# Up products of three of eleven pairs of inner tiles as seven products of halves

## The chip, the cores and the metric

The kernel runs on one core of one Trainium2 chip. The metric is the device time of one execution in microseconds (us), the median of several runs. The core has a matrix engine (TensorE: PE for its products, PEld for its weight loads), a vector engine (VectorE, DVE), a scalar engine (ScalarE, ACT), GpSimd (POOL) and SyncE (SP), which issues the transfers.

## The reference, cut to what matters

One decoder layer on 512 tokens of width 1024: forgetting attention with 16 heads, layer norm, a gated MLP with a causal convolution, layer norm, and a gated embedding. The change lies in the MLP:

```python
def conv_ffn(x, w_up, conv_w, conv_b, w_down):      # x: 512 x 1024, FFN_DIM = 2816
    u, g = jnp.split(x @ w_up, [FFN_DIM], axis=-1)
    g = causal_dwconv(g, conv_w, conv_b)             # three taps along the tokens
    return (jax.nn.gelu(g, approximate=False) * u) @ w_down
```

## The kernel before, in words

Every operand of a product is float32 and is cut into a high and a low part (`whi`, `wlo`); `three` (L113, its matmul is L118) makes one product from three matmuls: high by high, high by low, low by high. Each matmul loads its own 128 x 128 weights.

`Weights` holds all weights of the kernel as one list of units in the order of their use. `load_to` (L70) issues a unit's transfer into one of four `raw` buffers; `cut_to` (L83) makes the high part on ACT (L96) and the low part on DVE (L97), into one of five pairs of split buffers; `get(i, 2)` asks for unit i with two more cut ahead of it. A unit may have a `make` function, which builds sums or differences of its blocks on DVE before the cut, with a second block that comes by its own transfer into a tile `side`.

The MLP has 22 inner tiles f of 128 columns, that is 11 pairs j = (2j, 2j+1). For each f, `up(f, 0)` computes the gate product g and `up(f, 1)` the product u: 8 blocks of 128 rows by three matmuls of 512 tokens, 24 matmuls in all, into one PSUM buffer (two buffers with the tag "two" from f = 6 on; the other six hold the down products). Only f = 0 and the gate of f = 1 go in halves of 256 tokens. `conv` (L572) reads g on ACT and DVE, and `product` (L583) multiplies by u into E, a tile of quarters of the pair's activations. After the second tile of a pair, `operands` (L588) makes four sums of the quarters on DVE and cuts seven quarters at once into `hh` and `hl` (L599, L600).

The down products of pairs 0 to 8 are already made as seven products of halves (the phases in `down`, L602), with the activations as the weights and 512 columns moving. Part p of the loop (L645) does the up products of six inner tiles; between them, `between` (L653) puts steps of the down products of the part before. A step is two products of 6 matmuls (one product in the last phase). What a phase has finished is added to y on DVE by `add_half` (L498, L501, L503), which frees its PSUM buffer. Pairs 9 and 10 (part 3) are done plainly at the end, in the stage r.

`flip` (L520) transposes x1, the normed input of the MLP, on PE into x1h and x1l.

The tile framework orders each engine's instructions when the program is built and inserts the waits; an instruction that waits holds up what stands behind it on its engine.

Of the kernel before, what the change touches and what calls it, by code (L numbers as in the profile page):

```python
# [9 lines left out]
F32 = mybir.dt.float32  # L10
F32R = mybir.dt.float32r
# [5 lines left out]
P = 128  # L17
# [12 lines left out]
REST = range(18, 22)  # L30

CHUNKS = (None, (1,) * 12, (1,) * 12, (2, 1) * 4)
HALF = S // 2
ALPHA = 2.0 ** 0.25
EPS = 1e-5
# [73 lines left out]
def trunk_layer(ctx: ExitStack, tc: tile.TileContext, xT, x2d, pT, wqk, wv0, wv1, wv2, bf, wo, wup, cwb,  # L109
# [44 lines left out]

    side = {}

    def down_units(part):
        def b_rows(j, k0, n, cols):  # L160
            return half_rows(wdn, 2 * j + k0, n, cols)

        def t12(j, i):
            def make(t):
                if t is None:
                    if part not in side:
                        side[part] = base.tile([P, 6, 512], F32, tag="xl", name=f"side{part}")
                    nc.sync.dma_start(side[part][:, i, :], wdn[2 * j * P:(2 * j + 1) * P, 0:512])
                    return None
                t1, t2 = t[:, :512], side[part][:, i, :]  # L170
                nc.vector.tensor_sub(t1, t1, t2)
                nc.vector.tensor_sub(t2, t[:, 512:], t1)
                return [t1, t2]
            return make

        def t3(t):
            if t is None:
                return None
            nc.vector.tensor_sub(t[:, :512], t[:, 512:], t[:, :512])
            return [t]  # L180

        def t4(i):
            def make(t):
                if t is None:
                    return None
                nc.vector.tensor_sub(t[:, :512], t[:, :512], side[part][:, i, :])
                return [t[:, :512]]
            return make

        js = PAIRS[part]  # L190
        return [(b_rows(j, 0, 2, 0), UNIT, None) for j in js] + \
            [(b_rows(j, 0, 2, 1), UNIT, t12(j, i)) for i, j in enumerate(js)] + \
            [(b_rows(j, 0, 2, 1), UNIT, t3) for j in js] + \
            [(b_rows(j, 1, 1, 0), 512, t4(i)) for i, j in enumerate(js)]

    u_up, u_dn = {}, [[] for _ in PAIRS]
    for part in range(4):
        fs = range(6 * part, min(6 * part + 6, NF))
        todo = down_units(part - 1) if part else []
        for i, (f, q) in enumerate((f, q) for f in fs for q in range(2)):  # L200
            u_up[f, q] = W.add(wup[f, 1 - q], inner=P)
            for _ in range(CHUNKS[part][i] if part else 0):
                if todo:
                    src, n, make = todo.pop(0)
                    u_dn[part - 1].append(W.add(src, n=n, inner=512, make=make))
# [311 lines left out]
        nc.vector.scalar_tensor_tensor(y[:, t], y[:, t], mv[:, 0:1], g, op0=ALU.subtract, op1=ALU.mult)  # L517
        nc.vector.scalar_tensor_tensor(y[:, t], y[:, t], mv[:, 3:4], b, op0=ALU.mult, op1=ALU.add)

    def flip(t, xh, xl):  # L520

        for n in range(2):
            ps = bank("nt")
            for k in range(4):
                nc.tensor.transpose(ps[:, k * P:(k + 1) * P],
                                    y[:, t, (4 * n + k) * P:(4 * n + k + 1) * P], ident)
            dst = slice(4 * n, 4 * n + 4), slice(t * P, (t + 1) * P)
            ps3 = ps.rearrange("p (k c) -> p k c", c=P)
            nc.scalar.activation(xh[:, dst[0], dst[1]], ps3, AF.Copy)
            nc.vector.tensor_sub(xl[:, dst[0], dst[1]], ps3, xh[:, dst[0], dst[1]].bitcast(F32))  # L530

    x1h = post.tile([P, KD, S], F32R, tag="xh", name="x1h")
    x1l = post.tile([P, KD, S], F32R, tag="xl", name="x1l")
    rows = ExitStack()
    rpool = rows.enter_context(tc.tile_pool(name="rows", bufs=1))
    g1, b1 = [row(rpool.tile([P, D], F32, name=n), src) for n, src in (("g1", gm), ("b1", bm))]
# [5 lines left out]
    for t in range(NT):  # L542
        ps = bank(f"ap{t}")
        tk = slice(t * P, (t + 1) * P)
        for k in range(KD):
            hi, lo = W.get(u_o[1][k // 2])
            c = slice(k % 2 * 512, k % 2 * 512 + 512)
            three(ps, hi[:, c], lo[:, c], oh[:, k, tk], ol[:, k, tk], k == 0, k == KD - 1,
                  weights_move=True)
            if t > 1 and k == 3:  # L550
                flip(t - 2, x1h, x1l)
        add_half(t, 1, ps, True)
        half_stats(t, 1)
        norm(t, g1, b1, (2, x1h, x1l) if t == 3 else None)
    rows.close()
    oT.close()

# [27 lines left out]

    gates = {}

    def operands(hh, hl, i, E):  # L588
# [10 lines left out]
        nc.scalar.activation(hh[:, i], E[:, HALF:], AF.Copy)  # L599
        nc.vector.tensor_sub(hl[:, i], E[:, HALF:], hh[:, i].bitcast(F32))  # L600

    def down(part, hh, hl):  # L602
# [4 lines left out]
        A11, A22, A12, S1, S2, S3, S4 = range(7)  # L607
        acc = {(b, i): bank(f"{b}{part}{i}", "six") for b in "yzx" for i in range(2)}
        seen, opened = set(), set()

        def chain(b, a, us, col, n):

            j, u = us[n]
            hi, lo = W.get(u, 2)
            last = n == k - 1
            c = slice(col * 512, col * 512 + 512)
            for i in range(2):
                tk = slice(a * HALF + i * P, a * HALF + (i + 1) * P)
                on = (b, i) in opened
                three(acc[b, i], hi[:, c], lo[:, c], hh[:, j, tk], hl[:, j, tk], n == 0 and not on,  # L620
                      last, weights_move=True, on=on)
                if last:
                    opened.add((b, i))
# [19 lines left out]

    before = None
    for part in range(4):  # L645
        if part < 3:
            shape = [P, len(PAIRS[0]), 7 * HALF]
        else:
            shape = [P, len(REST), S]
        hh, hl = [hpool.tile(shape, F32R, tag=g, name=f"{g}{part}", bufs=2) for g in ("hh", "hl")]  # L650
        slots = iter(CHUNKS[part] or ())

        def between():  # L653
            for _ in range(next(slots, 0)):
                next(before)

        for f in range(6 * part, min(6 * part + 6, NF)):
            q, j = f % 2, f // 2
            if q == 0:
                E = hpool.tile([P, 8 * HALF], F32, tag="E", name=f"E{j}")  # L660
            if f == 0:
                a, b = slice(0, HALF), slice(HALF, S)
                up(0, 0, a)
                up(0, 1, a)
                up(1, 0, a, (3, x1h, x1l))
# [6 lines left out]
            if f > 1:  # L672
                up(f, 0)
            conv(f)
            between()
            up(f, 1)
            product(f, E[:, q * S:(q + 1) * S])
            if q:
                if part < 3:
                    operands(hh, hl, j - 3 * part, E)  # L680
                else:
                    i = f - 1 - REST[0]
                    e = E[:, :2 * S].rearrange("p (a b) -> p a b", b=S)
                    nc.scalar.activation(hh[:, i:i + 2], e, AF.Copy)
                    nc.vector.tensor_sub(hl[:, i:i + 2], e, hh[:, i:i + 2].bitcast(F32))
            between()
        if part < 3:
            before = down(part, hh, hl)
# [4 lines left out]
    for g in ("hh", "hl"):  # L693
        extra.append(hpool.tile([P, 3, UNIT], F32R, tag=g, name=f"{g}p", bufs=2))
    for i, t in enumerate(tiles):
        tk = slice(t * P, (t + 1) * P)
        for n in range(2):
            ps = bank(f"r{t}_{n}", "six")
            for k in range(len(REST)):
                hi, lo = W.get(u_r[n][k // 2])  # L700
                c = slice(k % 2 * 512, k % 2 * 512 + 512)
                three(ps, hi[:, c], lo[:, c], hh[:, k, tk], hl[:, k, tk], k == 0, k == len(REST) - 1,
                      weights_move=True)
            add_half(t, n, ps, False)
            half_stats(t, n)
# [108 lines left out]
```

## Time and profile before

| | |
|---|---|
| median of 3 runs | 660.29 us (660.05 to 661.29) |
| the profiled execution | 662.73 us, of which the span from first to last instruction is 661.0 us |
| busy in the span: PE, PEld | 653.7 us (99%), 556.8 us (84%) |
| busy in the span: DVE, ACT, POOL | 474.6 us (72%), 309.5 us (47%), 84.2 us (13%) |
| granted TensorE clock | 0.996 of full speed |
| DMA | 76.95 MB, mean 116 GB/s |

A busy PE is read from pipelined records, so that 99% says that matmuls follow each other without holes, not that each runs at its peak. Idle time of an engine that isn't the bottleneck costs nothing. The MLP's up and down products run from 249 to 576 us.

### The profile page before, as it was taken

Reading aid. Unit: us, or ns where it says so; the run is one execution under the profiler, and the core shown is the slowest. Engines: PE = TensorE matmul, PEld = TensorE weight load, DVE = VectorE, ACT = ScalarE, POOL = GpSimd, SP = SyncE. Lnnn points to the kernel's source line nnn. Section 1 sums busy time; section 2 is a strip of 40 time slices with the busy share of each in tenths; the row PEclk is TensorE's granted clock in tenths of the full one; section 3 lists DMA queues with packets and bytes.
Section 4 is the critical chain, followed back from the end, with each engine's and each line's share of the span. In section 5 each row is a group of like instructions: output and inputs, shape, how many; then the busy total and the mean of one; then the engine's idle time right before and its main releaser. Section 6 shows DMA issues by size and latency. Waiting matters only on the chain.

```text
span 661.0 us, 8683 instructions
## 1 busy us (share of the span) xinstructions
PE 653.7 (99%) x3234; PEld 556.8 (84%) x3234; DVE 474.6 (72%) x746; ACT 309.5 (47%) x511; POOL 84.2 (13%) x78
## 2 busy tenths in 40 slices
PE   8999999999999999999999999999999999999997
PEld 6899888888888889888888888888888888888886
DVE  6574789988896597755677675777657766599364
ACT  5543777877776223534434333443425343426231
POOL 0000544454446020000000000000000000012000
PEclk8999999999999999999999999999999999999999
DMA  8533211122153213323344244533363433562221
GB/s 281 168 125 115 82 46 54 65 65 65 37 208 125 98 36 125 128 97 95 98 140 146 95 160 128 159 128 112 100 199 117 125 133 125 159 224 66 101 81 48
DMA packets 32890, 76.95 MB, mean 116 GB/s; under 512 B 2960, under 2 KB 6800, under 8 KB 32848
## 3 DMA queue, kind: packets, MB, share of 16 engines
q1 hardware_dynamic: 32848, 76.41, 36.0%
q8 instruction: 25, 0.41, 0.3%
q14 instruction: 17, 0.14, 0.1%
HBM read 74.17 MB, written 2.10 MB: 115 GB/s over the span
## 4 chain that ended last, share of the span: by engine, by line
PE 97%; DMA 1%; ACT 1%; SPq 0%; issue 0%; DVE 0%
PE g L118 18%; PE u L118 18%; PE pp L118 13%; PE x L118 7%; PE pv L118 7%; PE gt L118 7%; PE z L118 4%; PE ao L118 3%; PE r L118 3%; PE ap L118 3%; PE o L408 3%; PE t L395 2%; PE y L118 2%; PE pl L118 2%; PE s L364 2%; PE s L366 1%
## 5 line engine op out<-in xcount | busy, mean ns | idle before, releaser
L96 ACT ACTIVATE whi<-raw 128x1024 fp32r<-128x1024 f32 (+5 forms) x131 | 126.3, 964 | 190.5 <-PE g L118 64.4
L97 DVE TENSOR_TENSOR wlo<-raw,whi 128x1024 fp32r<-128x1024 f32 (+5 forms) x131 | 143.3, 1099 | 67.4 <-ACT whi L96 67.0
L382 POOL TENSOR_SCALAR pr<-pr,rl 128x128 f32<-128x128 f32 (+1 forms) x64 | 71.9, 1141 | 138.1 <-DVE rl L378 138.1
L118 PE MATMUL g<-x1h,whi 128*128 128x512 f32 (+1 forms) x192 | 71.5, 372 | 0.0
L118 PE MATMUL g<-x1l,whi 128*128 128x512 f32 (+1 forms) x192 | 71.3, 371 | 0.0
L118 PE MATMUL g<-x1h,wlo 128*128 128x512 f32 (+1 forms) x192 | 71.3, 371 | 0.0
L118 PE MATMUL u<-x1h,whi 128*128 128x512 f32 (+1 forms) x184 | 69.9, 380 | 0.0
L118 PE MATMUL u<-x1l,whi 128*128 128x512 f32 (+1 forms) x184 | 69.9, 380 | 0.0
L118 PE MATMUL u<-x1h,wlo 128*128 128x512 f32 (+1 forms) x184 | 69.9, 380 | 0.0
L514 POOL TENSOR_TENSOR mv<-mv,neghalf 128x1 f32<-128x1 f32 x8 | 11.6, 1446 | 382.6 <-DVE mv L513 360.3
L118 PE MATMUL pp<-xh,wlo 128*128 128x512 f32 x128 | 50.5, 394 | 0.0
L118 PE MATMUL pp<-xl,whi 128*128 128x512 f32 x128 | 50.0, 390 | 0.0
L118 PE MATMUL pp<-xh,whi 128*128 128x512 f32 x128 | 49.9, 390 | 0.0
L374 ACT ACTIVATE pr<-s,nm 128x128 f32<-128x128 f32 (+1 forms) x64 | 33.4, 524 | 17.4 <-DVE nm L373 14.3
L118 PEld LDWEIGHTS g<-x1h,wlo 128*128 128x128 f32 x192 | 36.2, 188 | 6.3
L118 PEld LDWEIGHTS g<-x1l,whi 128*128 128x128 f32 x192 | 36.2, 188 | 6.2
L118 PEld LDWEIGHTS g<-x1h,whi 128*128 128x128 f32 x192 | 36.1, 188 | 6.2
L584 DVE TENSOR_TENSOR E<-a,u 128x512 f32<-128x512 f32 x22 | 15.1, 686 | 35.8 <-PE u L118 35.1
L118 PEld LDWEIGHTS u<-x1h,wlo 128*128 128x128 f32 x184 | 34.6, 188 | 6.6
L118 PEld LDWEIGHTS u<-x1h,whi 128*128 128x128 f32 x184 | 34.6, 188 | 6.5
L118 PEld LDWEIGHTS u<-x1l,whi 128*128 128x128 f32 x184 | 34.6, 188 | 6.5
L118 PE MATMUL pv<-whi,xh 128*128 128x384 f32 (+1 forms) x96 | 30.6, 331 | 1.9 <-ACT whi L96 1.9
(173 smaller groups left out, 1420.0 us busy)
## 6 DMA issues: line engine op xcount, KB each, us to landing
raw<-wup SPq DMA_DIRECT2D x44, 512.0 KB
raw<-wdn SPq DMA_DIRECT2D x31, 512.0 KB
raw<-wqk SPq DMA_DIRECT2D x16, 512.0 KB
raw<-wo SPq DMA_DIRECT2D x8, 512.0 KB
raw<-wg SPq DMA_DIRECT2D x8, 512.0 KB
raw<-wv SPq DMA_DIRECT2D x8, 384.0 KB
side<-wdn SPq DMA_DIRECT2D x9, 256.0 KB
raw<-wdn SPq DMA_DIRECT2D x9, 256.0 KB
```

The source lines that it names most:

```text
L96: self.nc.scalar.activation(hi[:, c:e], piece, AF.Copy)
L97: self.nc.vector.tensor_sub(lo[:, c:e], piece, hi[:, c:e].bitcast(F32))
L118: nc.tensor.matmul(ps, lhsT, rhs, start=start and n == 0, stop=stop and n == 2, skip_group_check=on)
L364: nc.tensor.matmul(ps[:, :n], QA[:, q], KA[:, :n], start=True, stop=False)
L366: nc.tensor.matmul(ps[:, :n], qb[0:68, q], kb[0:68, :n], start=False, stop=True)
L374: nc.scalar.activation(pr[:, off:off + w], ps[:, :w], AF.Exp, bias=nm[:, i:i + 1], accum_out=ls[:, i:i + 1])
L382: nc.gpsimd.tensor_scalar_mul(pr[:, off:off + w], pr[:, off:off + w], rl[:, i:i + 1])
L395: nc.tensor.transpose(ps[:, w:w + P], pr[:, o:o + P], ident)
L408: nc.tensor.matmul(ps[:, q0:], V[:, j, h], p[:, o:o + w], start=j == 0 and n == 0, stop=j == NT - 1 and n == 1)
L514: nc.gpsimd.tensor_tensor(mv[:, 3:4], mv[:, 2:3], neghalf, op=ALU.pow)
L584: nc.vector.tensor_mul(e, gates.pop(f), ups.pop((f, 1)))
```

## The change

For the pairs j = 4, 7 and 9, the two gate products (and likewise the two u products) are made as one 2 x 2 block product by Strassen's scheme in Winograd's form: the blocks are two halves of the 1024 rows by the two inner tiles for the weights, and two halves of the tokens by two halves of the rows for x1. Seven block products of 4 x 3 matmuls with 256 moving tokens take the place of eight. The sums of x1's blocks are made once, after f = 1 (`x_sums`), from an uncut copy of x1^T which `flip` now also writes (`whole`), and stay resident in `xs`. The sums of the weights' blocks are made by DVE in the units' `make` functions (`up_units`). A pair's seven products go in four stages of `up_step`, first for s = 0 (the gate), then for s = 1, with steps of the down products between them; partial sums leave PSUM by ACT (c1, c2) and return by DVE additions into E. `conv` and `product` of these pairs read E.

The down products' operands lie in three kinds of tiles (A, B, S) by how long they live instead of `hh` and `hl`, so that `operands` cuts them by three instructions on each engine instead of one. The tile `side` is one for the whole kernel.

```diff
+UP_PAIRS = (4, 7, 9)
...
+    def up_units(j):
+        f0, f1 = 2 * j, 2 * j + 1
+
+        def unit(f, q, make=None, k0=0):
+            return W.add(wup[f, 1 - q][:, k0:], n=(KD - k0) * P, inner=P, make=make)
+
+        return (lambda q: unit(f0, q), lambda q: unit(f1, q, t12(wup[f0, 1 - q][:, :4], 3 + q)),
+                lambda q: unit(f1, q, t3), lambda q: unit(f0, q, t4(3 + q), 4))
...
-        for i, (f, q) in enumerate((f, q) for f in fs for q in range(2)):
-            u_up[f, q] = W.add(wup[f, 1 - q], inner=P)
+        for i in range(2 * len(fs)):
+            f, q = fs[i // 2], i % 2
+            j, n = f // 2, i % 4
+            if j in UP_PAIRS:
+                stages = up_units(j)
+                for st, sq in (((0, 0),), ((0, 1),), ((1, 0), (1, 1)), ((2, 0), (2, 1)))[n]:
+                    u_up[j, st, sq] = stages[st](sq)
+            else:
+                u_up[f, q] = W.add(wup[f, 1 - q], inner=P)
...
+            if j in UP_PAIRS and n == 3:
+                for sq in range(2):
+                    u_up[j, 3, sq] = stages[3](sq)
...
-    def flip(t, xh, xl):
+    def flip(t, xh, xl, whole=None):
...
+        for k, ps3 in halves if whole is not None else ():
+            nc.scalar.activation(whole[t][:, k, :], ps3, AF.Copy)
...
+    def x_sums():
...
+        for i in range(2):
+            nc.vector.tensor_add(s(0, i), blk(2 + i, 0), blk(2 + i, 1))
+            nc.vector.tensor_sub(s(1, i), s(0, i), blk(i, 0))
+            nc.vector.tensor_sub(s(2, i), blk(i, 0), blk(2 + i, 0))
+            nc.vector.tensor_sub(s(3, i), blk(i, 1), s(1, i))
+        for n in range(4):
+            k = slice(4 * n, 4 * n + 4)
+            nc.scalar.activation(xs[0][:, k, :], sums[n], AF.Copy)
+            nc.vector.tensor_sub(xs[1][:, k, :], sums[n], xs[0][:, k, :].bitcast(F32))
+
+    def up_step(j, st, s, E):
+        if st == 0:
+            ups[j, s] = bank(f"{'gu'[s]}{2 * j}", "two" if j > 2 else None)
+        ps = ups[j, s]
+        z, x = ps[:, :HALF], ps[:, HALF:]
+        hi, lo = W.get(u_up[j, st, s], 2)
...
+        def go(to, col, on, a=None, sn=None, last=4):
+            for k in range(4):
+                w = slice((4 * col + k) * P, (4 * col + k + 1) * P)
+                if a is None:
+                    mh, ml = [v[:, 4 * sn + k, :] for v in xs]
+                else:
+                    mh, ml = [v[:, a[0] + k, a[1]] for v in (x1h, x1l)]
+                three(to, hi[:, w], lo[:, w], mh, ml, k == 0 and not on, k == 3, on=on)
...
+        if st == 0:
+            go(z, 1, False, a=(4, first))
+            go(x, 0, True, a=(0, first))
+            nc.scalar.activation(c1, z, AF.Copy)
+            nc.scalar.activation(z.rearrange("p (a b) -> p a b", b=P),
+                                 zeros.unsqueeze(1).to_broadcast([P, 2, P]), AF.Copy)
+            nc.vector.tensor_add(e[:, :HALF], x, c1)
+        elif st == 1:
+            go(z, 0, True, sn=0)
+            go(x, 1, True, sn=1)
+            nc.scalar.activation(c2[:, :HALF], x, AF.Copy)
+            nc.scalar.activation(c2[:, HALF:], z, AF.Copy)
+        elif st == 2:
+            go(z, 1, True, sn=3)
+            go(x, 0, True, sn=2)
+            nc.vector.tensor_add(e[:, S:], ps, c2)
+        else:
+            go(x, 0, True, a=(4, second))
+            nc.scalar.activation(e[:, HALF:S], x, AF.Copy)
+            del ups[j, s]
...
+            if j in UP_PAIRS:
+                if q == 0:
+                    up_step(j, 0, 0, E)
+                    between()
+                    up_step(j, 0, 1, E)
+                    between()
+                    continue
+                for st in (1, 2):
+                    up_step(j, st, 0, E)
+                    up_step(j, st, 1, E)
+                    if st == 1:
+                        between()
+                conv_product(f, E)
+                between()
+                up_step(j, 3, 0, E)
+                up_step(j, 3, 1, E)
+                conv_product(f - 1, E)
...
+            if f == 1:
+                x_sums()
```

## Rows read from the trace of the kernel before

**Rows 1.** The page, part 1: engine, busy us, share of the span, instructions.
```profile
PE 653.7 (99%) x3234; PEld 556.8 (84%) x3234; DVE 474.6 (72%) x746; ACT 309.5 (47%) x511; POOL 84.2 (13%) x78
```
**Rows 2.** The page, part 4: the chain that ended last, by engine.
```profile
PE 97%; DMA 1%; ACT 1%; SPq 0%; issue 0%; DVE 0%
```
**Rows 3.** Windows of whole pairs: length, busy us (instructions) of each engine, clock, DMA.
```profile
316.56:349.20 32.64, 32.64 (x146) 27.03 (x145) 24.87 (x36) 12.96 (x17) 0.00 (x0) 1.00 0.37 114
349.20:381.84 32.64, 32.64 (x146) 27.03 (x145) 22.18 (x29) 12.25 (x14) 0.00 (x0) 1.00 0.35 114
381.84:410.40 28.56, 28.56 (x128) 23.65 (x127) 17.04 (x22) 11.72 (x14) 0.00 (x0) 1.00 0.52 164
443.04:475.68 32.64, 32.64 (x146) 27.03 (x145) 22.27 (x29) 12.25 (x14) 0.00 (x0) 1.00 0.36 114
504.24:542.32 38.08, 38.08 (x170) 31.53 (x169) 28.81 (x40) 15.40 (x19) 0.00 (x0) 1.00 0.42 131
542.32:576.32 34.00, 34.00 (x152) 28.15 (x151) 21.67 (x28) 12.98 (x16) 0.00 (x0) 1.00 0.44 136
```
**Rows 4.** Waits from 316.56 to 576.32: who waited for whom, us, times, longest.
```profile
ACT whi L96 <- PE g L118: 51.5, 15, 4.8
ACT whi L96 <- PE u L118: 51.0, 17, 4.8
```
**Rows 5.** Timeline of PE, first and last matmul of the first half of u0.
```profile
252.31 0.28 PE L118 MATMUL u<-x1h,whi 128*128 128x256 f32 x1
...
255.07 0.28 PE L118 MATMUL u<-x1h,wlo 128*128 128x256 f32 x1
```
**Rows 6.** Timeline of PE: first matmul of a gate product and what follows its 24.
```profile
349.20 0.39 PE L118 MATMUL g<-x1h,whi 128*128 128x512 f32 x1
...
354.64 0.39 PE L118 MATMUL z<-whi,hh 128*128 128x512 f32 x1
```
**Rows 7.** The page, part 5: one group of weight loads.
```profile
L118 PEld LDWEIGHTS g<-x1h,wlo 128*128 128x128 f32 x192 | 36.2, 188 | 6.3
```
**Rows 8.** Groups of DVE by line and form: busy us, mean ns, idle before.
```profile
L97 DVE TENSOR_TENSOR wlo<-raw,whi 128x1024 fp32r<-128x1024 f32 x99 | 120.1, 1218 | 55.8 <-ACT whi L96 55.5
L600 DVE TENSOR_TENSOR hl<-E,hh 128x1792 fp32r<-128x1792 f32 x9 | 18.2, 2021 | 5.9 <-ACT hh L599 5.9
...
L97 DVE TENSOR_TENSOR wlo<-raw,whi 128x512 fp32r<-128x512 f32 x18 | 12.3, 685 | 5.6 <-ACT whi L96 5.6
L503 DVE TENSOR_TENSOR y<-y,x 128x512 f32<-128x512 f32 x18 | 12.0, 680 | 0.0
...
L171 DVE TENSOR_TENSOR raw<-raw,side 128x512 f32<-128x512 f32 x9 | 6.2, 690 | 7.0 <-DMA raw<-wdn 7.0
...
L598 DVE TENSOR_TENSOR E<-E 128x256 f32<-128x256 f32 x9 | 3.8, 423 | 0.2
```
**Rows 9.** Groups of ACT by line and form.
```profile
L96 ACT ACTIVATE whi<-raw 128x1024 fp32r<-128x1024 f32 x99 | 104.9, 1059 | 133.4 <-PE g L118 50.1 <-PE u L118 26.7 <-PE z L118 9.0
...
L307 ACT ACTIVATE V<-pv 128x256 fp32r<-128x256 f32 x4 | 1.4, 420 | 0.0
```
**Rows 10.** Timeline of ACT where the gate product of rows 6 ends.
```profile
354.61 1.06 ACT L96 ACTIVATE whi<-raw 128x1024 fp32r<-128x1024 f32 x1 [2.78 <-PE g L118]
355.58 0.76 ACT L576 ACTIVATE a<-g,cw 128x512 f32<-128x512 f32 x1
```
**Rows 11.** Timelines of SP and of DVE: a transfer's issue, and what waited for it.
```profile
332.69 0.38 SPq L77 DMA_DIRECT2D raw<-wdn  x1
...
336.57 0.69 DVE L171 TENSOR_TENSOR raw<-raw,side 128x512 f32<-128x512 f32 x1 [1.22 <-DMA raw<-wdn]
```
**Rows 12.** Windows, columns as in rows 3: from u2 to u5, and in stage r.
```profile
278.48:316.56 38.08, 38.08 (x170) 31.53 (x169) 21.58 (x25) 14.32 (x17) 0.00 (x0) 1.00 0.30 97
576.32:592.82 16.50, 16.50 (x73) 13.39 (x72) 16.21 (x23) 4.59 (x5) 1.46 (x1) 1.00 0.70 231
```

More of the change, by code (lines that the diff above doesn't have):

```diff
@@ L153, in trunk_layer, with side, t12, make @@
     u_o = [[W.add(half_rows(wo, 2 * j, 2, n), inner=512) for j in range(4)] for n in range(2)]
-    side = {}
+    aside = []
+    def side(i):
+        if not aside:
+            aside.append(base.tile([P, 8, 512], F32, tag="xl", name="side"))
+        return aside[0][:, i, :]
+    def t12(b11, i):
+        def make(t):
+            if t is None:
+                to = side(i)
+                if len(b11.shape) == 3:
+                    to = to.rearrange("p (a b) -> p a b", b=P)
+                nc.sync.dma_start(to, b11)
+                return None
+            t1, t2 = t[:, :512], side(i)
+            nc.vector.tensor_sub(t1, t1, t2)
+            nc.vector.tensor_sub(t2, t[:, 512:], t1)
+            return [t1, t2]
+        return make
+    def t3(t):
+        if t is None:
+            return None
+        nc.vector.tensor_sub(t[:, :512], t[:, 512:], t[:, :512])
+        return [t]
+    def t4(i):
+        def make(t):
+            if t is None:
+                return None
+            nc.vector.tensor_sub(t[:, :512], t[:, :512], side(i))
+            return [t[:, :512]]
+        return make
     def down_units(part):
@@ L518, in norm @@
         nc.vector.scalar_tensor_tensor(y[:, t], y[:, t], mv[:, 3:4], b, op0=ALU.mult, op1=ALU.add)
-    def flip(t, xh, xl):
+    def flip(t, xh, xl, whole=None):
+        halves = []
         for n in range(2):
@@ L530, in flip, with cut_tiles @@
             nc.vector.tensor_sub(xl[:, dst[0], dst[1]], ps3, xh[:, dst[0], dst[1]].bitcast(F32))
+            halves.append((dst[0], ps3))
+        for k, ps3 in halves if whole is not None else ():
+            nc.scalar.activation(whole[t][:, k, :], ps3, AF.Copy)
     x1h = post.tile([P, KD, S], F32R, tag="xh", name="x1h")
     x1l = post.tile([P, KD, S], F32R, tag="xl", name="x1l")
+    post.tile([P, 48], F32, name="lead")
+    spool = ctx.enter_context(tc.tile_pool(name="spool", bufs=1))
+    def cut_tiles(kind, n, bufs, name, dtype=F32R, pool=spool):
+        return [pool.tile([P, n, HALF], dtype, tag=f"{kind}{g}", name=f"{name}{g}", bufs=bufs) for g in "hl"]
+    xt, sums = {}, []
+    for t in range(NT):
+        a, b = cut_tiles("S", 4, 4, f"x1t{t}", F32)
+        xt[t] = a.rearrange("p a (b c) -> p (a b) c", c=P)
+        sums.append(b)
     rows = ExitStack()
@@ L586, in trunk_layer, with blk, s @@
     gates = {}
-    def operands(hh, hl, i, E):
+    xs = cut_tiles("X", 16, 1, "xs", pool=hpool)
+    def x_sums():
+        def blk(t, k):
+            return xt[t][:, 4 * k:4 * k + 4, :]
+        def s(n, i):
+            return sums[n][:, :, i * P:(i + 1) * P]
+        for i in range(2):
[7 more added lines that the diff above has]
+            nc.vector.tensor_sub(xs[1][:, k, :], sums[n], xs[0][:, k, :].bitcast(F32))
@@ L591, in e, with conv_product, operands @@
+    def conv_product(f, E):
+        c = slice(f % 2 * S, f % 2 * S + S)
+        ups[f, 0], ups[f, 1] = E[:, 2 * S:][:, c], E[:, c]
+        conv(f)
+        product(f, E[:, c])
+    def operands(ops, E):
         def e(n):
@@ L616, in chain @@
             c = slice(col * 512, col * 512 + 512)
+            xh, xl = ops[j][a[0]]
             for i in range(2):
-                tk = slice(a * HALF + i * P, a * HALF + (i + 1) * P)
+                tk = slice(i * P, (i + 1) * P)
                 on = (b, i) in opened
-                three(acc[b, i], hi[:, c], lo[:, c], hh[:, j, tk], hl[:, j, tk], n == 0 and not on,
+                three(acc[b, i], hi[:, c], lo[:, c], xh[:, a[1], tk], xl[:, a[1], tk], n == 0 and not on,
                       last, weights_move=True, on=on)
@@ L645, in trunk_layer @@
     for part in range(4):
[L646 to L650, printed above, removed]
+        ops = []
         slots = iter(CHUNKS[part] or ())
@@ L671, in trunk_layer @@
                 continue
[L672 to L677, printed above, removed]
+            if j in UP_PAIRS:
[15 more added lines that the diff above has]
+                conv_product(f - 1, E)
+            else:
+                if f > 1:
+                    up(f, 0)
+                conv(f)
+                between()
+                up(f, 1)
+                product(f, E[:, q * S:(q + 1) * S])
+            if f == 1:
+                x_sums()
             if q:
                 if part < 3:
-                    operands(hh, hl, j - 3 * part, E)
-                else:
[L682 to L686, printed above, removed]
+                    ops.append([cut_tiles("A", 2, 3, f"a{j}"), cut_tiles("B", 1, 5, f"b{j}", pool=hpool),
+                                cut_tiles("S", 4, 4, f"s{j}")])
+                    operands(ops[-1], E)
+                else:
+                    h, l = cut_tiles("S", 4, 4, f"s{j}")
+                    e = E[:, :2 * S].rearrange("p (a b) -> p a b", b=HALF)
+                    nc.scalar.activation(h, e, AF.Copy)
+                    nc.vector.tensor_sub(l, e, h.bitcast(F32))
+                    ops.append((h, l))
+            if j not in UP_PAIRS:
+                between()
         if part < 3:
-            before = down(part, hh, hl)
+            before = down(part, ops)
     gb = hpool.tile([P, 2, D], F32, tag="E", name="g2b2")
```

59 lines of the change are left out of this document (21 added, 38 removed).

## The prediction

> **What bounds the kernel now.** I read the page's first part, then the chain that ended last, then windows of single pairs. PE is busy in 99% of the span [rows 1] and makes 97% of the chain [rows 2]; in every window of the MLP its busy time is the window itself, at the full clock of 2.4 GHz [rows 3]. So a saved PE microsecond is a saved microsecond as long as nothing else takes its place, and every stall of PE counts in full. Next comes DVE: in the windows of j = 3, 4, 7, 9 and 10 it is busy 24.87 of 32.64, 22.18 of 32.64, 22.27 of 32.64, 28.81 of 38.08 and 21.67 of 34.00 us [rows 3]. Idle DVE there isn't lateness. The longest waits of the MLP are ACT's, for PE to give back a split buffer (51.5 and 51.0 us in 32 times) [rows 4]: cutting runs as far ahead as five split buffers allow, one in use and four ready. That lead is what the change will draw on.
>
> **PE's part.** In halves of 256 tokens, 24 matmuls follow each other at (255.07 - 252.31) / 23 = 0.120 us [rows 5]. With 512 tokens 24 take 354.64 - 349.20 = 5.44 us, 0.2267 each [rows 6]. The columns alone are 106.7 and 213.3 ns at 2.4 GHz, so each matmul has 13.3 ns on top, whatever its width. A pair before: 2 tiles x 2 products x 24 = 96 wide matmuls, 21.76 us. After: 2 x 7 x 12 = 168 narrow ones, 20.16 us. An eighth fewer columns would be 2.72 us, but 72 more matmuls take 0.96 back; 1.60 us are left, in three pairs 4.80. This is the only time removed from the path. The down products have the same number and width of matmuls.
>
> The narrow row above has its own weight load for each matmul, and was taken while DVE was busy too. The Trainium skill ("TensorE: Matmul & The Clock Gate", "Back-to-back issue gap") gives a lone warm matmul N / 2.4 + 2.5 ns. By that a pair would go from 20.72 to 18.35 us, and the three would save 7.1. The trace doesn't agree: it has 13.3 ns where the page has 2.5, and I take the row.
>
> **DVE's part, in a changed pair.** Durations from [rows 8]: a plain unit's low part 1.22 us, 512 columns 0.685, a sum of 512 columns 0.69, of 256 0.42. Before, four up units took 4 x 1.22 = 4.87. After, for each of g and u: stage 0 1.22; stage 1 two sums and two cuts, 2.75; stage 2 a sum and a full cut, 1.91; stage 3 a sum and half a cut, 1.37; together 7.25, for both 14.50, so 9.6 more. The partial sums into E add 2 x 0.42 + 2 x 0.69 = 2.2. Three operand cuts in place of one of 2.02 cost 0.685 + 0.42 + 1.22 = 2.3, so 0.3 more (not for j = 9, which has no such operands). Pairs 4, 7 and 9 then need 34.3, 34.4 and 40.6 us of DVE, and PE takes 31.04, 31.04 and 36.48. DVE is over by 3.3, 3.4 and 4.2: in these pairs it, not PE, is the slower engine. Whether that shows is a question of the lead.
>
> I followed it for j = 4 by hand, from PE's start of stage 0 as time 0. Order of use: A (stage 0, s = 0), a down step, B, a down step d5, C and D (stage 1), d6, E and F (stage 2), d7, G and H (stage 3); PE gives A to F 2.88 us each, G and H 1.44, a down step 2.72. Five split buffers mean that A, B and the first down step are cut at 0. The last u product of j = 3 ended at -2.72; its product and operands (0.69 + 1.7 + 2.3 us) hold DVE until 2.0. Then DVE finishes d5 at 4.7, C (with A's addition to E) at 7.9, D at 10.6, d6 (with B's) at 12.9, four additions to y (0.68 each) at 15.7, E at 17.6, F at 19.5, d7 at 21.4, G at 22.8, H at 24.1. PE wants C at 11.2, D 14.1, d6 17.0, E 19.7, F 22.6, d7 25.4, G 28.2, H 29.6. The least margin is 2.1 us, at E; each cut here also starts after its buffer is free. For j = 9 (two down steps, then one, in turn) the same gives E finished at 23.6 and wanted at 25.1: 1.5 us. So the lead covers the overrun, and the following pair, with 34.00 - 21.67 = 12.3 idle us after j = 9 and 28.56 - 17.04 = 11.5 after j = 4 [rows 3], pays it back. I cost DVE's excess at nothing, with its full 3.3 + 3.4 + 4.2 = 10.9 us as the upper bound if that cover were gone.
>
> **x_sums and whole.** Eight sums of 512 and four cuts of 1024 columns: 8 x 0.69 + 4 x 1.22 = 10.4 us of DVE after f = 1. From u2 to u5 DVE idles 38.08 - 21.58 = 16.5 us [rows 12], and the sums aren't used before j = 4. Cost nothing. Without that cover, product, sums and operands would stand in a row for 15.1 us; f = 2 gives 10.9 us of PE, so a unit for f = 3 still uncut (1.2 more) would hold PE 5.4 us. ACT's eight copies from the transposes and four high parts, 8 x 0.6 + 4 x 1.06 = 9 us, have ACT's idle time.
>
> **ACT.** Per changed pair: 8.0 us of high parts where there were 4.2 (a 1024 one is 1.06), and ten copies of 256 columns at 0.42 [rows 9], together 8 to 8.5 more on 12.25 of 32.64 [rows 3]. ACT stays at two thirds.
>
> **Hand-backs in PSUM.** A stage's next product into the same buffer waits for ACT or DVE to have read it. After A, B, C, D and E at least 5.6 us of PE work stand in between, after F 4.2; a chain of three copies and additions is 1.3. The short one is after G: the next pair's g product wants the buffer 1.44 us later. ACT takes a cut first, as it does before a conv: the cut starts at 354.61, the conv's first step at 355.58 [rows 10]. That is 0.97 + 0.42 = 1.39 us for the copy's end. I take 0.1 us a pair, 0.3 in all; bounds 0 and a second cut of 1.06 before it, 3.2 in all.
>
> **Transfers.** A changed pair loads 4 MB for the up products where it was 2. j = 4 moves 114 GB/s x 32.64 us = 3.7 MB now, so 5.8 in 31 us, 188 GB/s; 231 were moved in stage r [rows 12]. From an issue at 332.69 to its use at 336.57 a transfer needs up to 3.9 us [rows 11], four raw buffers deep. Cost nothing; if late, the price is that of late weights below. The `side` block adds one issue on SP before the next raw, under 0.4 us each. The operand tiles by lifetime remove no wait of PE, as there is none, and each is written after its buffer's last reader in PE's order: nothing either way.
>
> **Sum.** Own time 662.73 - 4.80 + 0.3 = 658.2 us. This execution lies 2.44 above the median of 660.29; so the median becomes 655.8. No change can be told within 0.2%, 1.3 us.
>
> **Rivals.** (1) DVE becomes the bound: its order puts sums or operands ahead of the cut that PE wants next, and the overrun reaches PE. In full: 660.29 - 4.80 + 10.9 = 666.4, slower. It decides once more than 1.6 us a pair reach PE, that is when the lead is 3.7 us short of what I followed at E (2.1 + 1.6). For it: 110% load, and margins of 1.5 to 2.1. Against: eleven us of lead and idle pairs behind. Chance 0.13 (0.02 of it no change).
> (2) Partial stalls, a buffer of PSUM or a unit late by about a cut in each pair: up to 3.2 us back, 656.5 to 659, mostly still faster. Chance 0.18 (0.04 no change).
> (3) x_sums as one burst: 660.29 - 4.80 + 5.4 = 660.9, no change. Chance 0.04.
> (4) The products don't shrink, since a weight load (188 ns in its record [rows 7]) is not hidden behind a narrow matmul: 168 x 0.188 = 31.6 us a pair, +9.8 each, 689.8. The row of 0.120 us with a load for each speaks against it. Chance 0.02. The Trainium skill (same page, "Measured speedup vs the span model") says that a load overlaps running matmuls only in another row group; by that rule this rival would hold, and the trace, whose loads fill all rows, doesn't agree.
> (5) The 13.3 ns don't recur and 7.1 are saved, by the page's rule above: 653.2. Chance 0.03.
>
> **How the numbers follow.** The forecast, all of the 4.8 with less than 1 us of stalls, has 0.60, and 655 to 656.5 as its own range. Faster: 0.60 + 0.14 + 0.03 = 0.77; no change 0.02 + 0.04 + 0.04 = 0.10; slower 0.11 + 0.02 = 0.13. The range leaves out rivals (4) and (5) and the slower part of (1), and the last of (3): from 654.8, just under PE's bound of 655.5, to 660.0.
>
> **What would show it.** In the changed profile: narrow matmuls in pairs 4, 7 and 9 at 0.120 us; those pairs, with their down steps, in 31.0, 31.0 and 36.5 us; DVE over 95% busy in them and PE waiting for `wlo`, E or a PSUM buffer for less than 0.3 us a pair; the x_sums lines scattered between 260 and 316 us. Wrong would be: PE idle at stage 2 with DVE as releaser (rival 1), PE idle at the first g product after stage 3 with ACT as releaser (rival 2), an idle PE at about 284 us (rival 3).

## The result, and the profile after

The changed kernel takes 663.48 us (median of 9 runs, 662.76 to 666.15), the kernel before, run beside it, 660.63 (9 runs, 659.82 to 661.29). The ratio is 1.0047, with a 95% interval of 1.0034 to 1.0060: the change makes the kernel 0.5% slower, where 655.8 us, a gain of 0.7%, was forecast. The profiled execution took 664.42 us, its span 662.7.

The page's parts 1 and 4 answer to [rows 1, 2].

```profile
PE 650.9 (98%) x3450; PEld 563.4 (85%) x3450; DVE 514.3 (78%) x830; ACT 339.2 (51%) x589; POOL 84.3 (13%) x78
```
```profile
PE 88%; DMA 4%; DVE 4%; ACT 2%; issue 2%; SPq 0%; ACTq 0%; DVEq 0%
```

PE has 2.8 us less to do and the span is 1.7 us longer. Twelve per cent of the chain, where it was three, are now not PE's but DMA's, DVE's, ACT's and issue. Where, the windows of the three changed pairs, of pair 10 and of stage r say (they answer to [rows 3, 12]):

```profile
347.02:379.42 32.40, 31.27 (x217) 29.10 (x215) 26.53 (x39) 16.89 (x28) 0.00 (x0) 1.00 0.53 168
...
440.78:472.50 31.72, 31.27 (x218) 29.10 (x216) 26.44 (x39) 16.90 (x28) 0.00 (x0) 1.00 0.52 171
501.20:540.64 39.44, 36.94 (x241) 33.66 (x239) 34.69 (x55) 19.90 (x34) 0.00 (x0) 1.00 0.47 148
540.64:576.40 35.76, 35.76 (x151) 29.40 (x151) 25.68 (x32) 14.27 (x18) 0.00 (x0) 0.95 0.47 147
576.40:594.70 18.30, 16.75 (x74) 13.31 (x73) 16.94 (x24) 4.96 (x5) 2.37 (x2) 1.00 0.72 245
```

The pairs take 32.40, 31.72 and 39.44 us where 31.04, 31.04 and 36.48 were worked out; pair 10 takes 35.76 at a granted clock of 0.95, where it took 34.00; r takes 18.30, where it took 16.50. From the first gate product to the first product of r the MLP takes 576.40 - 247.17 = 329.2 us, before 576.32 - 249.35 = 327.0. (That it began 2.2 us earlier here has nothing to do with the change: in the runs below it begins between 246.2 and 248.0.) The view of waits names PE's releasers:

```profile
PE g L120 <- ACT E L697: 3.4, 3, 1.8
PE r L120 <- ACT s10h L824: 1.6, 1, 1.6
...
PE u L120 <- DVE E L694: 0.7, 1, 0.7
```

The letters A to H name a pair's up products as in the prediction (G and H are the two of stage 3, for g and for u); "into E" means the tile E. PE's timeline: the last product of pair 4's stage 3, the two of pair 9, and r's first product of pair 10's operands.

```profile
376.69 0.28 PE L120 MATMUL u<-x1h,whi 128*128 128x256 f32 x1
...
379.42 0.50 PE L120 MATMUL g<-x1h,whi 128*128 128x512 f32 x1 [1.13 <-ACT E L697]
...
534.88 0.28 PE L120 MATMUL g<-x1h,whi 128*128 128x256 f32 x1
...
536.19 0.28 PE L120 MATMUL g<-x1h,wlo 128*128 128x256 f32 x1
537.19 0.36 PE L120 MATMUL u<-x1h,whi 128*128 128x256 f32 x1 [0.72 <-DVE E L694]
...
540.64 0.50 PE L120 MATMUL g<-x1h,whi 128*128 128x512 f32 x1 [1.78 <-ACT E L697]
...
579.47 0.50 PE L120 MATMUL r<-whi,s10h 128*128 128x512 f32 x1 [1.55 <-ACT s10h L824]
```

Twelve narrow matmuls follow each other at (536.19 - 534.88) / 11 = 0.119 us: PE's part is as forecast, and a product of stage 3 should take 1.44 us. From start to start, H of pair 4 took 379.42 - 376.69 = 2.73. A wait costs a little more than the idle time that it is listed with: the first matmul behind it has a longer record (0.50 us at 379.42 and 540.64, where 0.39 is usual), and the next starts 0.1 us late. So the ledger goes by starts: time over 1.44 (narrow) and 5.44 (the wide product behind it).

| place | us lost |
|---|---|
| PE waits for ACT's copy of G, pairs 4, 7, 9 | 1.44 + 0.76 + 2.15 = 4.35 |
| PE waits for DVE's addition into E, pair 9 (536.3 to 537.2) | 0.88 |
| granted clock at 1.2 GHz in pair 10's first product | 1.61 |
| left over in the MLP | 0.22 |
| stage r, PE waits for `s10h` | 1.8 |

In the MLP that is 7.06 us, which is just 329.22 - (326.96 - 4.80); the 0.22 left over are put to no place.

**The copy of G.** ACT's timeline at the end of pair 4; PE began H, the product after G, at 376.69:

```profile
376.49 0.63 ACT L630 ACTIVATE a<-a 128x512 f32<-128x512 f32 x1 [2.78 <-DVE a L628]
377.02 1.04 ACT L98 ACTIVATE whi<-raw 128x1024 fp32r<-128x1024 f32 x1
378.16 0.42 ACT L720 ACTIVATE b4h<-E 128x256 fp32r<-128x256 f32 x1
378.49 0.61 ACT L98 ACTIVATE whi<-raw 128x512 fp32r<-128x512 f32 x1
379.01 0.36 ACT L697 ACTIVATE E<-g 128x256 f32<-128x256 f32 x1
```

The copy (L697), 0.36 us long, stands behind a GELU that has waited 2.78 us for DVE's half of the convolution, and behind two cuts and an operand's copy that could not start before the GELU. ACT was idle for those 2.78 us; its busy share (16.89 of 32.40) tells nothing of this. The order on ACT is the one that the program was built with. The Trainium skill ("PSUM — Partial Sum Buffer", "Engine vs sequencer instructions") says that the queues of ScalarE and VectorE are strictly first in, first out; the trace agrees: the copy, whose product was done when or soon after H began, started at 379.01.

DVE's half of the convolution was late in its turn. Ahead of it, in pairs 4 and 7, stood a sum of weights that waited for its transfer:

```profile
372.64 0.69 DVE L192 TENSOR_TENSOR raw<-raw,side 128x512 f32<-128x512 f32 x1 [2.12 <-DMA raw<-wdn]
...
465.71 0.69 DVE L192 TENSOR_TENSOR raw<-raw,side 128x512 f32<-128x512 f32 x1 [1.43 <-DMA raw<-wdn]
```

Such waits are not new: between 247 and 577 us DVE waits 20.8 us for transfers of weights, and 18.8 in the kernel before, where they cost nothing. New is what stands behind them. No run brought the transfers earlier, so what part of the 4.35 us is theirs is not shown.

**The addition into E.** DVE's timeline in pair 9; PE had left F for the down step at 532.13:

```profile
533.96 0.69 DVE L185 TENSOR_TENSOR raw<-raw 128x512 f32<-128x512 f32 x1 [1.95 <-DMA raw<-wdn]
534.57 1.22 DVE L99 TENSOR_TENSOR wlo<-raw,whi 128x1024 fp32r<-128x1024 f32 x1
535.70 0.74 DVE L626 SCALAR_TENSOR_TENSOR a<-E,cw,a 128x511 f32<-128x511 f32 x1
536.37 0.68 DVE L694 TENSOR_TENSOR E<-u,side 128x512 f32<-128x512 f32 x1
536.97 0.74 DVE L628 SCALAR_TENSOR_TENSOR a<-E,cw,a 128x510 f32<-128x510 f32 x1
```

A sum of weights for a later step waits 1.95 us for its transfer. A cut, a step of a convolution, the addition for which PE waits, and the second step, for which ACT's GELU waits, stand behind it; so this transfer, too, delays both the addition and G's copy.

**Stage r.** ACT's timeline where r begins:

```profile
576.47 1.06 ACT L98 ACTIVATE moreh<-raw 128x1024 fp32r<-128x1024 f32 x1 [2.51 <-DMA raw<-wpl]
577.43 1.04 ACT L98 ACTIVATE whi<-raw 128x1024 fp32r<-128x1024 f32 x1
578.38 1.04 ACT L824 ACTIVATE s10h<-E 128x1024 fp32r<-128x1024 f32 x1
```

In the kernel before, the operand copy (there `hh`) stood ahead of the three cuts for the embedding (`hhp`):

```profile
575.95 1.06 ACT L684 ACTIVATE hh<-E 128x1024 fp32r<-128x1024 f32 x1
576.91 2.94 ACT L96 ACTIVATE hhp<-raw 128x1024 fp32r<-128x1024 f32 x3
```

By the code those cuts went into the buffer that the last down products read; now they go into the place of `xs`, whose last reader is in pair 9, so they may start earlier. The order puts two of them, one with a transfer that lands 2.51 us late, ahead of the copy that PE wants.

**The clock.** Windows of 1 us behind pair 9's stalls, and two starts of wide matmuls in them:

```profile
541.00:542.00 1.00, 1.00 (x5) 0.82 (x4) 1.00 (x2) 0.71 (x2) 0.00 (x0) 0.74 0.00 0
542.00:543.00 1.00, 1.00 (x4) 0.81 (x3) 1.00 (x2) 0.00 (x0) 0.00 (x0) 0.50 0.25 37
...
545.00:546.00 1.00, 1.00 (x6) 0.80 (x5) 1.00 (x2) 0.48 (x1) 0.00 (x0) 1.00 0.58 174
```
```profile
541.83 0.63 PE L120 MATMUL g<-x1l,whi 128*128 128x512 f32 x1
...
544.39 0.63 PE L120 MATMUL g<-x1l,whi 128*128 128x512 f32 x1
```

From 536.5 to 540.6 PE had done one narrow product in four us; then, 0.8 us into pair 10's first product (the mean of 0.74 in the first window), the granted clock fell to 0.50, 1.2 GHz, for 3.4 us.

### The profile page after: what moved, and what is told of

The parts are those of the page before. It is cut to its first block, busy times and chain, and to the rows that moved or that the text cites. A ratio compares the mean times of both kernels' runs of the same rounds, so it can differ in the third digit from the quotient of the medians.

```text
span 662.7 us, 9314 instructions
## 1 busy us (share of the span) xinstructions
PE 650.9 (98%) x3450; PEld 563.4 (85%) x3450; DVE 514.3 (78%) x830; ACT 339.2 (51%) x589; POOL 84.3 (13%) x78
## 4 chain that ended last, share of the span: by engine, by line
PE 88%; DMA 4%; DVE 4%; ACT 2%; issue 2%; SPq 0%; ACTq 0%; DVEq 0%
PE g L120 16%; PE u L120 15%; PE pp L120 13%; PE gt L120 7%; PE pv L120 6%; PE x L120 6%; PE ao L120 3%; PE ap L120 3%; PE o L440 3%; PE r L120 3%; PE z L120 3%; PE t L427 2%; DMA raw<-wdn 2%; DVE wlo L99 2%; PE pl L120 2%
## 5 line engine op out<-in xcount | busy, mean ns | idle before, releaser
L98 ACT ACTIVATE whi<-raw 128x1024 fp32r<-128x1024 f32 (+5 forms) x143 | 133.3, 934 | 136.7 <-PE g L120 44.4
L99 DVE TENSOR_TENSOR wlo<-raw,whi 128x1024 fp32r<-128x1024 f32 (+5 forms) x143 | 151.4, 1065 | 53.9 <-ACT whi L98 53.7
L120 PE MATMUL g<-x1h,whi 128*128 128x512 f32 (+1 forms) x180 | 64.0, 355 | 3.4 <-ACT E L697 3.4
L120 PE MATMUL g<-x1l,whi 128*128 128x512 f32 (+1 forms) x180 | 63.5, 353 | 0.0
L120 PE MATMUL g<-x1h,wlo 128*128 128x512 f32 (+1 forms) x180 | 63.4, 352 | 0.0
L120 PE MATMUL u<-x1h,whi 128*128 128x512 f32 (+1 forms) x172 | 61.5, 357 | 0.7 <-DVE E L694 0.7
L120 PE MATMUL u<-x1l,whi 128*128 128x512 f32 (+1 forms) x172 | 61.4, 357 | 0.0
L120 PE MATMUL u<-x1h,wlo 128*128 128x512 f32 (+1 forms) x172 | 61.4, 357 | 0.0
L120 PEld LDWEIGHTS u<-x1h,whi 128*128 128x128 f32 x172 | 32.5, 189 | 5.6 <-issue 0.9
L630 ACT ACTIVATE a<-a 128x512 f32<-128x512 f32 x22 | 13.9, 631 | 34.8 <-DVE a L628 34.8
```

Source lines behind the costliest of these rows:

```text
L98: self.nc.scalar.activation(hi[:, c:e], piece, AF.Copy)
L99: self.nc.vector.tensor_sub(lo[:, c:e], piece, hi[:, c:e].bitcast(F32))
L120: nc.tensor.matmul(ps, lhsT, rhs, start=start and n == 0, stop=stop and n == 2, skip_group_check=on)
L630: nc.scalar.activation(a, a, AF.Gelu)
```

## The experiments

"Pairs" are the changed ones; "MLP" is the time from the first gate product to the first product of r in the profiled execution. Kernel before: 660.43 us (e1 to e4), 660.54 (e5 to e8), 660.58 (e9 to e12).

| run | us, median | ratio (95%) | MLP | r |
|---|---|---|---|---|
| e1 no pairs | 661.93 | 1.0023 (1.0014 to 1.0032) | 326.96 | 18.43 |
| e2 pairs 4, 7 | 661.82 | 1.0029 (1.0017 to 1.0041) | 326.57 | 17.48 |
| e3 r in order | 661.61 | 1.0019 (1.0007 to 1.0031) | 328.45 | 16.50 |
| e4 gap | 657.21 | 0.9958 (0.9945 to 0.9970) | 322.72 | 18.41 |
| e5 gap, r | 657.07 | 0.9946 (0.9933 to 0.9958) | 324.02 | 16.51 |
| e6 conv behind | 658.14 | 0.9972 (0.9962 to 0.9982) | 324.58 | 17.74 |
| e7 no sums | 658.85 | 0.9980 (0.9970 to 0.9990) | 324.32 | 17.51 |
| e8 pairs 3, 5, 7, 9 | 654.70 | 0.9915 (0.9901 to 0.9928) | 321.36 | 16.50 |
| e9 addition first | 656.69 | 0.9945 (0.9932 to 0.9959) | 323.33 | 16.50 |
| e10 four, addition first | 655.19 | 0.9921 (0.9908 to 0.9935) | 321.89 | 16.50 |
| e11 five pairs | 656.52 | 0.9935 (0.9921 to 0.9948) | 322.98 | 16.50 |
| e12 after again | 661.50 (one run) | | 326.56 | 18.02 |

**e1, e2: fewer pairs.** `UP_PAIRS = ()`, and `UP_PAIRS = (4, 7)`.

> All of the change but the seven products: no pair is changed, x_sums and the uncut copy are still made, the operand tiles are the new ones. Theory A (the losses are places in ACT's and DVE's fixed order; the one at the start of the stage r comes from the new tile for the embedding's parts, which lets ACT take their cuts ahead of s10h): no loss in the up products, and still 1.5 to 2 us at the start of r, so 662.0 to 662.7. Theory B (DVE has too much work in the changed pairs, and what is left over delays r): no loss anywhere, 660.6. Theory C (x_sums or the uncut copy cost time at the start): a loss before 285 us.

> Pairs 4 and 7 changed, pair 9 not. Theory A: two times 1.60 us saved, 1.4 and 0.8 us lost at the hand-backs after stage 3, and 1.8 us at r: 660.6 - 3.2 + 2.2 + 1.8 = 661.4. Theory B: without pair 9 nothing is left over for r, 659.6. If the fall of the clock after pair 9 is the one heavy loss, this is 2 us below the changed kernel in both.

Without any changed pair the MLP takes 326.96 us, as before: the sums of x1 and the new operand tiles cost it nothing. The whole is 1.5 us slower all the same, and one wait stands in the MLP and r that wasn't there before:

```profile
PE r L120 <- ACT s10h L824: 1.7, 1, 1.7
```

So the 1.8 us of r belong to the new tiles (of the operands and, with them, of the embedding's parts) and not to the changed pairs. e2's ten runs spread from 660.57 to 663.86, and its profile is of the fastest. With pairs 4 and 7 3.2 us should be saved in the MLP, and 0.4 are: the copies of G take back 1.87 and 0.73.

**e3: stage r in order.** The three cuts of the embedding's weights stand behind `s10h` on ACT.

```diff
+            if home is not None and self.behind is not None:
+                with self.tc.issue_after(self.behind):
+                    self.nc.scalar.activation(hi[:, :n], t[:, :n], AF.Copy)
...
-                    nc.scalar.activation(h, e, AF.Copy)
+                    W.behind = nc.scalar.activation(h, e, AF.Copy).ins
```

> The changed kernel, with the three cuts of the embedding's parts queued on ACT behind the high part of the last operands, s10h. Theory A: the 1.8 us at the start of r vanish, 661.7. Theory B: s10h is late by itself, no change, 663.5.

r takes 16.50 us again, and no wait of it is left: that cause is shown. In the MLP the waits stand as in the changed kernel (pair 9: F's addition 0.88, H 3.45 us from start to start, as there), but the clock did not fall behind them: the next product took 5.58 us, not 7.19.

**e4, e5: a down step between G and H.** The down step that stood before stage 3 comes between its two products, in the order of the weights' units too; e5 is e4 with e3.

```diff
                 conv_product(f, E)
-                between()
                 up_step(j, 3, 0, E)
+                between()
                 up_step(j, 3, 1, E)
```

> The changed kernel, with the down step that stood before stage 3 put between its two products, so that PE has 4.2 us of work instead of 1.4 between a stage-3 product and the next product into the same PSUM buffer. Theory A: the waits for ACT's last copy (1.1, 0.5 and 1.8 us), most of the slow product before them and the fall of the clock that follows the third (1.7 us) vanish, 658 to 659. Theory B, or late transfers: the same work is still late on DVE, the wait moves to the next unit's low part or to the addition into E, 662 or more.

> The edits of e4 and of e3 together. Theory A says that they mend two separate places: e4's 657.2 less the 1.7 to 1.9 us at the start of r, so 655.3 to 655.6, which is the 655.5 at which PE alone would set the time. If the two are one backlog, it stays at 656.5 or more.

e4 is 6.3 us under the changed kernel: all three waits for G's copy are gone, with no operation less on ACT or DVE. One wait of PE is left in the MLP and r:

```profile
PE r L120 <- ACT s10h L825: 1.7, 1, 1.7
```

In e5 r is mended as well, but it is 1.5 us short of what was expected. Its profile has one wait in the MLP, of 1.3 us, for pair 9's first addition of stage 2 (L704); DVE:

```profile
530.10 0.69 DVE L194 TENSOR_TENSOR raw<-raw 128x512 f32<-128x512 f32 x1 [2.02 <-DMA raw<-wdn]
530.71 0.68 DVE L704 TENSOR_TENSOR E<-g,side 128x512 f32<-128x512 f32 x1
```

It is what happened in the changed kernel's pair 9, at the other addition. The edit has a part in it: with the down step gone from before G, G wants E's addition after F's 2.88 us alone, where it had 5.6. In e4 the same place lost 0.27 us.

**e6: the convolution behind the copy.** The products in the changed kernel's order; the pair's first convolution and GELU stand behind H's copy.

```diff
-                conv_product(f, E)
                 between()
                 up_step(j, 3, 0, E)
-                up_step(j, 3, 1, E)
+                last = up_step(j, 3, 1, E)
+                with tc.issue_after(last):
+                    conv_product(f, E)
```

> The changed kernel with its order of products, but the conv and product of the pair's second tile queued behind the two last copies on ACT (no more PE work in between). Theory A, as far as it blames the GELU that waits in front of the copy: the waits at the next g product fall from 1.1, 0.5 and 1.8 us to 0.5 or less each, 659.5 to 661, r's 1.8 us stay. If the cuts in front of the copy, whose transfers land late, are what holds it up: waits as before, 663.

The waits for G's copy are gone here too, although G and H stand next to each other: it is what stood in the queue, the convolution with its waiting GELU, and not the short distance alone. ACT at the end of pair 4, where H starts at 376.42 and the next product at 377.86, and all of PE's waits in the MLP and r:

```profile
376.55 0.63 ACT L98 ACTIVATE whi<-raw 128x512 fp32r<-128x512 f32 x1 [0.48 <-PE g L120]
377.09 0.36 ACT L697 ACTIVATE E<-g 128x256 f32<-128x256 f32 x1
```
```profile
PE u L120 <- DVE E L694: 1.7, 1, 1.7
PE r L120 <- ACT s10h L826: 1.0, 1, 1.0
```

Pair 9 waits 1.7 us for the addition, behind a sum whose transfer is 1.97 late.

**e7: less work for DVE.** The block sums of the changed pairs' up weights are left out, so that these products are of other numbers; the additions into E, the convolutions and all transfers stay.

```diff
             t1, t2 = t[:, :512], side(i)
+            if i > 2:
+                return [t1, t2]
             nc.vector.tensor_sub(t1, t1, t2)
...
-                lambda q: unit(f1, q, t3), lambda q: unit(f0, q, t4(3 + q), 4))
+                lambda q: unit(f1, q), lambda q: unit(f0, q, t4(3 + q), 4))
...
+            if i < 3:
+                nc.vector.tensor_sub(t[:, :512], t[:, :512], side(i))
```

> The changed kernel without DVE's sums of the up weights' blocks (their raw blocks are cut and multiplied instead, so the products are of other numbers), 5.5 us of DVE less in each changed pair. Theory B: the losses of the pairs vanish, 657 to 658. Theory A: DVE's amount isn't the cause, the copies keep their places in the queue; at most a third goes, 661 to 663.

It comes out between the two: pair 9 loses nothing, pairs 4 and 7 still lose 0.72 and 1.04 to the copy. So pair 9's loss hangs on the sums, be it their load or their places in DVE's queue (the run doesn't separate these); the other two stay for the most part without them.

**e8: four pairs.** e5 with `UP_PAIRS = (3, 5, 7, 9)`.

> e5 with four changed pairs, 3, 5, 7 and 9, in place of 4, 7 and 9. Theory A: another 1.60 us, 653.9. If DVE's overrun has a limit near three pairs far apart (pairs 3, 5, 7 and 9 leave one plain pair between them, 10 to 12 us of idle DVE against 3.3 of overrun), a loss in the last of them, 655 or more.

This is the fastest kernel of the study, 0.85% under the one before. No wait of PE is listed in its MLP; 0.4 us is lost in pair 5's stage 1.

**e9, e10: the addition ahead of the sums.** e5 and e8, with the weight sums that are asked for after stage 2's first product queued behind its addition; for this the product asks for one unit ahead in place of two.

```diff
-        hi, lo = W.get(u_up[j, st, s], 2)
+        hi, lo = W.get(u_up[j, st, s], 1 if (st, s) == (2, 0) else 2)
+        W.hold = None
...
-            nc.vector.tensor_add(e[:, S:], ps, c2)
+            add = nc.vector.tensor_add(e[:, S:], ps, c2)
+            W.hold = add.ins if s == 0 else None
...
+            elif self.hold is not None:
+                with self.tc.issue_after(self.hold):
+                    pieces = make(t)
```

> Pairs 4, 7, 9 with the down step between the two last products and stage r's cuts in order (as the run before it of these two edits together, 657.07 us), and now the sums of down weights that follow stage 2 stand behind the gate's addition into E on DVE, where they stood in front of it in pair 9 and waited there for a transfer. Theory A (that place is what is left of the loss, a PE wait of 1.3 us): no wait of PE for E in pair 9, 655.5 to 656.0 us. Theory B (the transfers are late anyway, and PE waits for the cut of the down step in place of the addition): a wait of PE for wlo of about 1 us, and 656.8 to 657.5 us.

> The same with pairs 3, 5, 7, 9, where the version without this edit took 654.70 us and showed no wait of PE in the MLP. Theory A (the additions were in time there): 654.2 to 654.8 us, no change. Theory B (the order has more effects than that one wait): over 655.3 us.

In e9 the wait in pair 9 is gone, and PE waits for nothing that the view of waits lists in the MLP. But only 0.7 of its 1.56 us came back there, and 0.4 in the median, whose interval overlaps e5's. PE's timeline shows what else the edit did:

```profile
530.18 0.28 PE L136 MATMUL g<-x1l,whi 128*128 128x256 f32 x1
530.41 0.51 PE L136 MATMUL z<-whi,s8h 128*128 128x512 f32 x1
530.76 0.28 PE L136 MATMUL g<-x1h,wlo 128*128 128x256 f32 x1
...
531.95 0.40 PE L136 MATMUL z<-whi,s8l 128*128 128x512 f32 x1
```

The framework now orders one matmul of the down step into the middle of G. In each changed pair G and the down product behind it together take 0.2 to 0.3 us longer (3.15 where 2.83 would do, in pair 4), 0.9 in all. e10 pays that in four pairs and has nothing to win: 655.19, no better than e8.

**e11: five pairs.** e5 with `UP_PAIRS = (3, 4, 5, 7, 9)`.

> Pairs 3, 4, 5, 7, 9 with the two mended orders. Theory A (only places in the queues cost, not DVE's amount): 1.6 us under four pairs' 654.70, that is 653.1 us. Theory B (three changed pairs in a row are over DVE's rate, about 34 us of work in 31 of PE, with no idle pair behind them to pay it back): each of pairs 4 and 5 loses 1.6 to 3 us, 654.7 to 658 us, with PE waiting for E or wlo in them.

A fifth pair loses 1.8 us instead of gaining 1.6. Windows from pair 4 to the start of pair 5, and PE's waits:

```profile
343.00:376.00 33.00, 33.00 (x228) 30.77 (x227) 32.42 (x51) 19.92 (x35) 0.00 (x0) 1.00 0.52 171
376.00:390.00 14.00, 12.10 (x82) 10.80 (x82) 14.00 (x25) 7.33 (x13) 0.00 (x0) 1.00 0.44 146
```
```profile
PE g L128 <- ACT whi L106: 1.5, 1, 1.5
...
PE u L128 <- DVE E L704: 0.6, 1, 0.6
PE g L128 <- DVE wlo L107: 0.4, 1, 0.4
```

DVE is busy 46.42 of 47 us; at pair 5's stage 1 PE waits 1.5 and 0.4 us for weights. This is the first rival of the prediction, which three pairs with plain ones between them didn't meet.

**e12: the changed kernel once more.**

> The changed kernel once more, unaltered, for its profile. If the fall of the granted clock behind pair 9's stalls belongs to the kernel, the slice of pair 10 again shows 0.50 for some 3 us and the span is near 662.7 us; if it comes in some executions only, the same two waits of PE (about 0.7 and 1.8 us) stand there at full clock and the span is 1.5 to 2 us shorter.

The waits for G's copy recur (1.0, 0.85 and 1.84 us in the three H products, start to start over 1.44, and 0.13 to 0.17 behind each), the addition is in time and the clock doesn't fall: the MLP takes 326.56 us where it took 329.22. Its span is 2.9 us shorter, more than the 1.5 to 2 expected, since the late addition (0.88) did not recur either. This one run, 661.50 us, lies under the lowest of the nine, 662.76: what the places cost differs from execution to execution.

**The ledger of all runs.** The MLP of before less 1.60 a pair, plus the excess of each product's time, plus 0.2 to 0.4 that are put to no place, gives the MLP of each profile within 0.1 to 0.2 us: e3 322.16 + 6.07 + 0.2 = 328.4 (328.45), e6 322.16 + 2.11 + 0.2 = 324.5 (324.58), e8 320.56 + 0.40 + 0.3 = 321.3 (321.36).

## Why the prediction was wrong, step by step

**PE's 4.80 us: right.** The pitch is 0.119 to 0.120 us in all changed pairs and 0.2267 in the wide products, and e9, where PE waits for nothing, has an MLP 326.96 - 323.33 = 3.6 us shorter, with 0.9 us lost to its own side effect: 4.5 of the 4.80 are seen. The Trainium skill's two rules behind rivals 5 and 4 ("TensorE: Matmul & The Clock Gate": 2.5 ns on top of a warm matmul's columns, in "Back-to-back issue gap"; loads that overlap matmuls only in another row group, which stands in "The mechanism") don't agree with this profile either: 13.3 ns on top, and loads of 191 ns in their records behind narrow matmuls that follow each other at 0.120 us.

**The hand-back in PSUM: the step that failed.** "ACT takes a cut first, as it does before a conv ... I take 0.1 us a pair, 0.3 in all; bounds 0 and a second cut of 1.06 before it, 3.2 in all." It measured 4.35 us, above the upper bound (and 4.1 in e12). The place was right, and its sign in the profile too (rival 2). What was wrong is the question: I priced the copy by ACT's durations in front of it and left out that an instruction in front may itself wait. The pair's own GELU, which the code puts just before stage 3, waits for the convolution on DVE, and the cuts wait behind it. e4 and e6 show this from two sides: more distance, or the GELU behind the copy, and the 4.35 us are gone. With the GELU behind, ACT does take one cut first, as the prediction had it: in e6 G's copy ends 377.45 - 376.42 = 1.03 us after H's start, within the 1.44.

**"Nothing either way" for the operand tiles: wrong by 1.8 us.** I looked for waits that the tiles remove, and at each tile's last reader. I did not look at what an earlier free tile lets ACT take ahead of `s10h`. e1 has the loss without any changed pair, e3 mends it by order alone.

**DVE's excess at nothing: nearly right, with transfers at nothing the weak point.** Its 10.9 us did not reach PE. They were too many: records of DVE overlap (in pair 9 one starts at 536.37, takes 0.68 and is followed at 536.97), so that sums of durations overstate its work. The terms for the three pairs and `x_sums` come to 46.4 us, and DVE is busy 514.3 - 474.6 = 39.7 us longer. In the windows it is busy 26.53 of 32.40 and 26.44 of 31.72, not 34.3 of 31.0 and not over 95%; how much of a changed pair's work is done in the pairs beside it isn't shown. But not every DVE instruction may be late by the lead: the additions into E are wanted at once, and one stood behind a sum that waited for a transfer, 0.88 us in this profile, 1.5 in e5, 1.8 in e6 and none in e12. The prediction gave F's addition 4.2 us and a chain of three steps 1.3. I followed the cuts by hand and took transfers as on time, though [rows 8] and [rows 11] show DVE waiting for them; the margin of pair 9, 1.5 us, is less than the 2 us by which they were late. Why they are late is open. SP's transfers into `side` wait 13.8 us in all for DVE's last reader, in front of raw ones, where they waited 0.5 before; but DVE's own waits for transfers grew by 2 us only, and more raw buffers or another order of issue were not tried.

**x_sums, ACT's load:** right. No PE time is lost around the sums, and ACT stays half busy.

**The clock:** not in the sum at all; 1.61 us in the profiled execution, and none in e3's and e12's. Of the nine runs, the five with a granted clock of 0.993 to 0.997 take 662.83 to 666.15 us, the four with 0.999 take 662.76 to 663.48.

**The sum.** 660.63 - 4.80 + 4.35 + 0.88 + 0.2 + 1.8 = 663.1, with the losses of the one profiled execution; the median is 663.48. The run at the median had a granted clock of 0.999, so the 0.4 left are not shown to be the clock; they stay open. Partial stalls (rival 2) are what came, and they were not "mostly still faster": with r they outweigh the gain.

## What to carry to other kernels

When a change shortens the work between two uses of a buffer, list what stands in front of the releasing instruction on its engine, and for each of those what it waits for; a half-idle engine with a waiting instruction at its head is as late as a full one. When tiles are split or renamed, ask what may now go earlier, and whom it overtakes. The cheapest cures here were of order alone: a step of other work between the two uses, and three cuts queued behind one copy, were worth 6 us of 660. A wait that cost nothing can cost in full once something that is wanted at once stands behind it.

## What the runs showed of the hardware

The granted clock fell to 1.2 GHz in the middle of the kernel, for 3.4 us, after 4.1 us (536.5 to 540.6) in which PE was busy for 1.67; nearly the same stalls in e3 (2.32 and 3.45 us for the two products) were followed by full clock. At 1.2 GHz wide matmuls follow each other at (544.39 - 541.83) / 6 = 0.427 us, which is their 512 columns and nothing more: the 13.3 ns on top show at 2.4 GHz alone. The Trainium skill ("TensorE: Matmul & The Clock Gate", "Wait — 56ns, not 53.3ns?") also has a fixed cost that shows at 2.4 GHz only; its size there, 2.5 ns, is not this kernel's.
